# The first stage of a hybrid S5, attention and expert layer: a hand-laid order on three engines, whole fp32 operands in four projections, chunk products with swapped operands, and other pages

## The chip, the cores and the metric

The kernel runs on one core of a Trainium2 chip. The metric is the device time of one execution in microseconds (us). TensorE (PE, and PEld for its weight loads) does products and transposes, VectorE (DVE), ScalarE (ACT) and GpSimd (POOL) do elementwise work, and SyncE (SP) issues nearly all DMAs, in program order.

## The reference

One layer over 256 latent and 256 context tokens of width 1024. Cut to what matters here:

```python
# h = modulated RMSNorm; one projection, columns [S5 input 512 | K 128 | V 128 | Q 512 | gates 2048]
ug  = u.reshape(b, l, 32, 16)                       # 32 groups of 16 channels
bu  = einsum('blgp,gnp->blgn', ug, bbar)            # 64 complex states per group
h   = diag_scan(lbar, bu, h0, reverse)              # both directions, context state carried over
y  += einsum('blgn,gpn->blgp', h, cmat).real        # S5 read-out, then GLU
q, k = rms_normalised_and_rotated(q, k)             # 8 query heads, 2 key heads, 64 wide
attn = softmax(q k^T over latent and context keys) v
out  = (sigmoid gates merge both branches) @ w_out  # gated residual add
# sub-layer 2: modulated RMSNorm, top 4 of 32 experts, clamped SwiGLU, gated residual, final norm
```

Shift, scale and gate of both sub-layers come from one product of SiLU(c) with `w_mod` (1024 x 6144).

## The kernel before, in words

SBUF holds 24 pages of 1 MB (`pg0` to `pg23`). `load` (L90) issues a DMA on SP's queue and keeps program order, so the weights form one stream; a page is loaded again after `release` or `used`, when its last reader has ended. The experts at the end are 32 x 12 such pages.

The first stage, up to the expert blocks, goes like this. Two kinds of product are used. `mm` takes fp32 operands whole. `mm3` (L83) takes operands that `split` has parted into a high and a low fp32r half (ACT copies the high half at L62, DVE subtracts at L63) and makes three products. Transposes are L86.

1. The context and latent activations `hT` are modulated and split into `hH`, `hL`. U, the S5 input projection, has 32 products of 128x256 (4 column blocks, 2 sequences, 4 k-tiles) with whole operands, k < 4, and 32 split ones, k >= 4. K and V (`kv_proj`, 32 products of 128x256) and Q (`q_proj`, 16 products of 128x512) are split.
2. `v_tables`, `w_tables` and `scan_multipliers` build the S5 tables on DVE. `v_transposes` turns the tables on PE.
3. U goes through two rounds of 16 transposes (A, then U's scan layout), each with four copies on DVE. Then eight chunk steps: `chunk_in` does four products of 64x256 and a copy on ACT, and `chunk_T` turns the result with four transposes and copies it out with two half-height copies on DVE and two on ACT. `scan_up` and `scan_steps` are the scan on DVE.
4. A loop over u = 0 to 15 does one half of a gate column block each (`gate_mm`, 24 products of 128x256; `gate_split` supplies its weights), one tile of the modulation (`mod_tile`, four products of 32x512 with one page of `w_mod`, after which `mod_load` fills the page again), one `k_kernel` (24 small products of the S5 convolution kernel; a copy to `R` after each four), from u = 4 on one unit of attention (`attn`), and other pieces at set places (`P_...`). After the last `k_kernel`, at u == 7, `R` is written to DRAM (`Rd`, 8 DMAs). At u == 9 `kernel_in` reads it back as a block Toeplitz table `Kt` (16 DMAs). `readout` at u == 11 and 12 needs `Kt`.

The 16 modulation tiles use two pages in turn, 23 and 16: eight tiles stand ahead of the loop, eight in u = 0 to 7. A scheduler orders the instructions; `strict["on"]` pins PE's order to the program's from just ahead of the loop on (L1155), `strict["vec"]` that of DVE and ACT from the output projection on. The two functions that move most:

```python
    def mod_tile(reload=True):
        ...
        if reload:
            mod_load(p_)
...
    def kernel_in():
        for hf in range(2):
            for i in range(8):
                load(Kt[hf][16 * i:16 * i + 16],
                             Rd[:, 16 * hf:16 * hf + 16, 16 * (7 - i):16 * (7 - i) + 128])
```

Of the kernel before, what the change touches and what calls it, by code (L numbers as in the profile page):

```python
# [29 lines left out]
P_QT, P_K, P_M, P_A, P_S, P_RO, P_RT, P_GL, P_B, P_BS, P_BL, P_BP = 1, 0, 10, 4, 9, 11, 13, 15, 1, 3, 1, 3  # L30
# [3 lines left out]
def hybrid_block(ctx: ExitStack, tc: tile.TileContext, a: dict, out: bass.AP):  # L34
    nc = tc.nc
    V, S, G, T = nc.vector, nc.scalar, nc.gpsimd, nc.tensor
    SP = nc.sync

# [323 lines left out]
    def split_h(k, s, eng):  # L362
        split(hT[s][:, k:k + 2], hH[s][:, k:k + 2], hL[s][:, k:k + 2], eng)

    def mod0_rows(c):
        m0 = pg(9, 1024 + 256 * c, 256)
        V.tensor_copy(m0, pm0[c][:, 0:256])  # L367
# [176 lines left out]
    mod_load(23)  # L544


    Vt = [pg(p_).rearrange("p (g r m) -> p g r m", g=8, r=2) for p_ in (22, 2, 3, 14)]
    vpage = [8, 9, 8, 9]
# [42 lines left out]
    WR, WI = [], []  # L591

    def w_tables(qt):
        gs = slice(8 * qt, 8 * qt + 8)
        td = pg((19, 11, 12, 3)[qt], 0, 1024).rearrange("p (g j k) -> p g j k", g=8, j=8)
        for r, tab in ((0, WR), (1, WI)):
            tab.append(pg((18, 19, 11, 12)[qt], 1024 * r, 1024).rearrange("p (g j k) -> p g j k", g=8, j=8))
# [7 lines left out]
        V.tensor_mul(WR[qt], cc(0), lw(0))  # L605
        V.tensor_mul(td, cc(1), lw(1))
        V.tensor_add(WR[qt], WR[qt], td)
        V.tensor_mul(WI[qt], cc(1), lw(0))
        V.tensor_mul(td, cc(0), lw(1))
        V.tensor_sub(WI[qt], WI[qt], td)  # L610
# [25 lines left out]
    renew(12, "r")
    renew(11, "r")
    wuh, wul = [pg(p_).rearrange("p (k f) -> p k f", k=4) for p_ in (12, 11)]
    for k in range(4):
        split(wu[1][:, k], wuh[:, k], wul[:, k], V)  # L640
    last = mod0_rows(1)
    del held["m", 0], held["m", 1]
    with tc.issue_after(last.ins):
        v_tables(0)
        v_tables(1)
        scan_multipliers()
    u_proj(0)
    u_proj(1)
# [5 lines left out]
    u_proj(2)
    for s_ in range(2):
        for k in (0, 2):
            split_h(k, s_, V)
# [7 lines left out]
    v_tables(3)
    v_transposes(2)

    kv_ps, q_ps = [], []

    def kv_proj(i):  # L670
        b = bank(("kv", i))
        for t in range(2):
            for k in range(8):
                ts_ = slice(128 * t, 128 * t + 128)
                mm3(b[:, 256 * t:256 * t + 256], hH[i][:, k, ts_], hL[i][:, k, ts_], wkvh[:, k], wkvl[:, k],
                    k == 0, k == 7)
        kv_ps.append(b)
# [67 lines left out]
    for i in range(8):  # L745
# [4 lines left out]
        if i % 2:  # L750
            mod_tile()
# [983 lines left out]
```

## Time and profile before

| | |
|---|---|
| median of 3 runs | 1284.38 us (1282.16 to 1284.6) |
| profiled execution | 1285.06 us, its span 1283.4 us |
| mean granted TensorE clock | 0.981 |
| PE busy | 1167.6 us (91%) |
| DVE busy | 424.4 us (33%) |
| ACT busy | 197.3 us (15%) |
| DMA | 462.56 MB, mean 360 GB/s |
| chain that ended last | PE 44%, DMA 43%, DVE 9% |

The span runs from the first to the last instruction of the profiled execution; 1.66 us lie around it. Busy shares are means over stages with different limits, so a change in the first stage is read from that stage alone. In the rows, x is a count of instructions, and "idle before" is the idle time of an engine just ahead of a group with the work that ended it.

### The profile page before, as it was taken

The page shows a single profiled execution, that of the slowest core. Times are in us where ns is not written, and L with a number is a line of the kernel's source. Part 1 is how long each engine was busy: PE and PEld are TensorE (multiplying, and loading weights), DVE is VectorE, ACT ScalarE, POOL GpSimd, SP SyncE. Part 2 cuts the span into 40 slices and gives each one's busy share as a digit, 9 for nine tenths or more (in the row PEclk, how much of TensorE's full clock was granted, in tenths as well). Part 3 has the DMA queues.
Part 4 walks back from the last instruction along what each step waited for, and adds up shares of the span by engine and source line. Part 5 has one row for each costly group of instructions (what it writes and reads, how often), then busy time and mean ns, then how long its engine had stood idle before and what let it go on. Part 6 is the DMA issues. An engine that isn't in the chain of part 4 may idle for free.

```text
span 1283.4 us, 16161 instructions
## 1 busy us (share of the span) xinstructions
PE 1167.6 (91%) x6711; PEld 538.0 (42%) x6712; DVE 424.4 (33%) x923; ACT 197.3 (15%) x372; POOL 39.1 (3%) x47
## 2 busy tenths in 40 slices
PE   3889698899999999999999898989898989999986
PEld 2667477788543333333333232323232323233224
DVE  5999998474321112211121111211111111111211
ACT  3334346441110000000000000000000000000001
POOL 1130100011000000000000000000000000000000
PEclk9899899899999999999999999999999999999998
DMA  9934479679899999999999999999999999999996
GB/s 281 291 105 158 169 259 175 192 268 367 313 417 417 418 417 417 416 416 417 417 416 418 417 418 418 417 417 417 418 416 416 417 416 416 416 417 416 417 386 197
DMA packets 123104, 462.56 MB, mean 360 GB/s; under 512 B 20669, under 2 KB 46953, under 8 KB 88210
## 3 DMA queue, kind: packets, MB, share of 16 engines
q1 hardware_dynamic: 122562, 460.90, 92.3%
q8 instruction: 55, 0.90, 0.3%
q0 software_dynamic: 416, 0.56, 0.1%
q14 instruction: 23, 0.19, 0.0%
q10 hardware_dynamic: 48, 0.01, 0.0%
HBM read 459.89 MB, written 1.54 MB: 360 GB/s over the span
## 4 chain that ended last, share of the span: by engine, by line
PE 44%; DMA 43%; DVE 9%; issue 2%; SPq 1%; ACT 1%; POOL 0%; DVEq 0%; POOLq 0%; ACTq 0%
PE bk L83 41%; DMA pg<-in_w_gate_up_dram 30%; DMA pg<-in_w_down_dram 11%; PE bk L86 3%; DVE pg L63 2%; DMA pg<-Rd 2%; SPq L90 1%; DVE pg L853 0%; DVE pg L851 0%; DVE pg L854 0%; DVE pg L565 0%; DVE pg L568 0%; DVE pg L566 0%; DVE pg L564 0%; DVE pg L844 0%
## 5 line engine op out<-in xcount | busy, mean ns | idle before, releaser
L83 PE MATMUL bk<-pg,pg 128*64 128x512 f32 (+6 forms) x5344 | 996.4, 477 | 69.0 <-DMA pg<-in_w_down_dram 28.1
L83 PEld LDWEIGHTS bk<-pg,pg 128*64 128x64 f32 (+3 forms) x5344 | 447.4, 154 | 554.7 <-issue 349.9
L1472 DVE TENSOR_SCALAR pg<-bk 128x512 f32<-128x512 f32 x32 | 22.1, 692 | 291.2 <-PE bk L83 291.2
L1383 DVE TENSOR_TENSOR pg<-bk,shT 128x512 f32<-128x512 f32 x32 | 22.1, 692 | 266.4 <-PE bk L83 266.4
L86 PE MATMUL bk<-ident,pg 128*128 128x128 f32 x480 | 79.9, 292 | 18.6 <-DVE pg L367 4.2
L86 PEld LDWEIGHTS bk<-ident,pg 128*128 128x128 f32 x480 | 54.4, 145 | 85.8 <-issue 46.2
L1505 DVE TENSOR_TENSOR pg<-bk,pg 128x512 f32<-128x512 f32 x30 | 20.7, 691 | 189.2 <-PE bk L83 189.2
L1484 ACT ACTIVATE pg<-bk 128x256 f32<-128x256 f32 x32 | 12.3, 383 | 396.2 <-PE bk L86 396.2
L83 PE MATMUL bk<-pg 64*128 64x512 f32 (+1 forms) x368 | 70.4, 485 | 0.0
L1489 ACT ACTIVATE pg<-bk 128x512 f32<-128x512 f32 x32 | 19.1, 596 | 258.1 <-PE bk L86 258.1
L63 DVE TENSOR_TENSOR pg<-pg,pg 128x512 fp32r<-128x512 f32 (+3 forms) x63 | 50.6, 817 | 18.4 <-ACT pg L62 16.3
L62 ACT ACTIVATE pg<-pg 128x512 fp32r<-128x512 f32 (+3 forms) x63 | 44.0, 721 | 51.4 <-PE bk L83 40.7
L1473 ACT ACTIVATE pg<-pg 128x512 f32<-128x512 f32 x32 | 20.1, 629 | 186.1 <-DVE pg L1472 186.1
L83 PEld LDWEIGHTS bk<-pg 64*128 64x128 f32 (+1 forms) x368 | 19.9, 160 | 50.2 <-issue 50.2
L83 PE MATMUL bk<-pg,selB 128*64 128x512 bf16 (+1 forms) x196 | 33.9, 383 | 0.0
L83 PE MATMUL bk<-pg,scond 128*32 128x256 f32 (+1 forms) x256 | 28.6, 519 | 0.8 <-DMA pg<-in_w_mod_dram 0.6
L1589 POOL DMA_DIRECT2D pg<-g2d x2 | 1.3, 642 | 883.8 <-PE bk L83 883.8
L1474 DVE TENSOR_SCALAR pg<-bk 128x512 f32<-128x512 f32 x32 | 22.1, 692 | 5.3 <-PE bk L83 5.3
L1476 DVE SCALAR_TENSOR_TENSOR pg<-pg 128x512 f32<-128x512 f32 x32 | 22.1, 692 | 1.1
L1475 DVE TENSOR_TENSOR pg<-pg 128x512 f32<-128x512 f32 x32 | 21.8, 682 | 1.9 <-ACT pg L1473 1.8
L1480 DVE TENSOR_SCALAR pg<-iot,posp,gate 128x128 f32<-128x128 f32 x64 | 18.9, 339 | 0.0
L1373 DVE TENSOR_SCALAR pg<-iot,posp,rs 128x64 f32<-128x64 f32 x64 | 15.7, 306 | 0.1
(294 smaller groups left out, 422.5 us busy)
## 6 DMA issues: line engine op xcount, KB each, us to landing
pg<-in_w_gate_up_dram SPq DMA_DIRECT2D x256, 1024.0 KB, 20.0
pg<-in_w_down_dram SPq DMA_DIRECT2D x127, 1024.0 KB, 20.0
pg<-in_w_mod_dram SPq DMA_DIRECT2D x16, 1024.0 KB, 5.4
pg<-in_w_in_dram SPq DMA_DIRECT2D x13, 1024.0 KB, 7.3
pg<-in_w_mod_dram SPq DMA_DIRECT2D x16, 512.0 KB, 9.0
pg<-in_w_out_dram SPq DMA_DIRECT2D x4, 1024.0 KB, 11.9
pg<-Rd SPq DMA_DIRECT2D x16, 128.0 KB, 8.5
pg<-in_w_ssm_out_dram SPq DMA_DIRECT2D x2, 1024.0 KB
```

The lines of the kernel that those rows point to most:

```text
L62: S.activation(hi.bitcast(F32R), src, AF.Copy)
L63: eng.tensor_sub(lo.bitcast(F32R), src, hi)
L83: pinned(T.matmul(*ar, **kw))
L86: pinned(T.transpose(*ar))
L1383: pv_(V.tensor_add(xg[p % 2][:, 4 * half:4 * half + 4], pb.rearrange("p (k m) -> p k m", k=4), shk[:, 4 * half:4 * half + 4].unsqueeze(2). ...
L1472: pv_(V.tensor_scalar(gx, pgate, 7.0, None, op0=ALU.min))
L1473: pa_(S.activation(sx, gx, AF.Sigmoid, scale=1.702))
L1474: pv_(V.tensor_scalar(ux, pup, 7.0, -7.0, op0=ALU.min, op1=ALU.max))
L1475: pv_(V.tensor_mul(gx, gx, sx))
L1476: pv_(V.scalar_tensor_tensor(ux, ux, 1.0, gx, op0=ALU.add, op1=ALU.mult))
L1489: pa_(S.activation(dst, pmx, AF.Copy))
L1505: pv_(V.tensor_mul(yx, pdn, g2h))
```

## The change

PE, DVE and ACT keep the program's order from the U projection on (`Pinned`). U, K, V and Q use whole fp32 operands, so the splits of `wu[1]`, `wkv`, `wq` and of the context activations go; `hH` and `hL` remain for the latents, for the gates. A chunk is sixteen products of 64x64 whose operands are swapped, so that the scan layout comes out at once; `chunk_T` goes, and one copy each on DVE and ACT remains. The copies after the A and U transposes move from DVE to ACT. The modulation uses one page at a time (10 for the first six tiles, 15 for the last ten); six tiles stand ahead of the loop and ten in u = 0 to 9. The loop does two `k_kernel` in each of u = 0 to 3, rotates Q and K at u = 0 and 1, does `scan_up` at u == 2 and the scan's pieces in u = 3 to 8, writes `Rd` at u == 3 and reads it at u == 5 (before 7 and 9). Other pages are renamed to fit.

```diff
-P_QT, P_K, P_M, P_A, P_S, P_RO, P_RT, P_GL, P_B, P_BS, P_BL, P_BP = 1, 0, 10, 4, 9, 11, 13, 15, 1, 3, 1, 3
+P_QT, P_M, P_A, P_SU, P_S, P_RO, P_RT, P_GL, P_B, P_BS, P_BL, P_BP = 2, 10, 4, 3, 9, 11, 13, 15, 1, 3, 1, 3
...
+    V, S = Pinned(nc.vector), Pinned(nc.scalar)
...
-    hH, hL = [[pg(p_).rearrange("p (k t) -> p k t", k=8) for p_ in ps] for ps in ((13, 0), (10, 1))]
+    mod_load(10)
...
+    hH, hL = [pg(p_).rearrange("p (k t) -> p k t", k=8) for p_ in (0, 1)]
...
-    mod_load(23)
...
-            o = ub[q][:, 256 * s:256 * s + 256]
-            if k < 4:
-                mm(o, wu[0][:, k, f], hT[s][:, k], k == 0 and s == 0, False)
-            else:
-                mm3(o, wuh[:, k - 4, f], wul[:, k - 4, f], hH[s][:, k], hL[s][:, k], False, k == 7 and s == 1)
-
-    def u_proj(q):
-        for k in range(4, 8):
-            u_mm(q, k)
+            mm(ub[q][:, 256 * s:256 * s + 256], wu[k // 4][:, k % 4, f], hT[s][:, k], k == 0 and s == 0,
+               k == 7 and s == 1)
...
+    def kv_proj(i, t):
...
+        for k in range(8):
+            mm(kv_ps[i][:, 256 * t:256 * t + 256], hT[i][:, k, 128 * t:128 * t + 128], wkv[:, k], k == 0, k == 7)
...
+    def q_proj(t):
+        b = bank(("q", t))
+        for k in range(8):
+            mm(b, hT[1][:, k, 128 * t:128 * t + 128], wq[k // 4][:, k % 4], k == 0, k == 7)
...
+    def a_transposes():
...
+                S.activation(A[:, h, :, 4 * j4:4 * j4 + 4], b.rearrange("p (j g k) -> p g j k", j=4, g=8), AF.Copy)
...
+                S.activation(U[:, 4 * g4:4 * g4 + 4, :, h], b.rearrange("p (g q c) -> p g q c", g=4, q=4), AF.Copy)
...
+    def chunk(i):
...
+        for j in range(4):
+            g = 4 * i + j
+            for r in range(2):
+                for d in range(2):
+                    rhs = U[:, g % 8, g // 8]
+                    mm(b[64 * d:64 * d + 64, 128 * j + 64 * r:128 * j + 64 * r + 64],
+                       Vt[g // 8][:, g % 8, r, 64 * d:64 * d + 64], rhs[:, :, ::-1] if d else rhs, True, True)
+        bv = b.rearrange("p (g r h c) -> p h c r g", g=4, r=2, h=2)
+        V.tensor_copy(vv[0][:, :, :, 4 * i:4 * i + 4], bv[:, 0])
+        S.activation(vv[1][:, :, :, 4 * i:4 * i + 4], bv[:, 1], AF.Copy)
...
+    strict["on"] = strict["vec"] = True
+    for k in range(3):
         for q in range(4):
             u_mm(q, k)
         mod0_mm(1, k)
...
+    mod0_mm(1, 3)
+    mod0_copy(1)
...
+    v_tables(0)
+    v_tables(1)
+    for k in (4, 5):
+        for q in range(4):
+            u_mm(q, k)
...
-    split(wkv, wkvh, wkvl, V)
...
+    v_tables(2)
+    v_tables(3)
+    scan_multipliers()
+    for q in range(4):
+        u_mm(q, 6)
+        u_mm(q, 7)
+        u_out(q)
+    kv_proj(0, 0)
+    a_transposes()
     v_transposes(0)
-    v_tables(2)
-    u_proj(3)
...
-    split(wq[0], wqh[0], wql[0], V)
...
+    for i in range(8):
+        if i in (4, 6):
+            v_transposes(i // 2)
+        chunk(i)
+        if i == 1:
+            release(22)
+        if i == 2:
+            S.activation(hH.bitcast(F32R), hT[1], AF.Copy)
+        if i < 3:
+            w_tables(1)
+        elif i == 3:
+            V.tensor_sub(hL.bitcast(F32R), hT[1], hH)
+        else:
+            w_tables(2)
+        if i in (3, 5):
+            mod_tile()
     mod_tile()
...
-    split(wq[1], wqh[1], wql[1], V)
-    mod_load(16)
...
-    def chunk_in(i):
-        b = bank()
-        for j in range(2):
-            for e in range(2):
-                g = 4 * i + 2 * j + e
-                mm(b[64 * e:64 * e + 64, 256 * j:256 * j + 256],
-                   U[:, g % 8, g // 8].rearrange("p h c -> p (h c)"),
-                   Vt[g // 8][:, g % 8].rearrange("p r m -> p (r m)"), True, True)
-        vo = pg(7, 512 * (i % 2), 512)
-        S.activation(vo, b, AF.Copy)
...
-    def chunk_T(i, vo):
-        b = bank()
-        for j in range(2):
-            for r in range(2):
-                ttrans(b[:, 128 * (2 * r + j):128 * (2 * r + j) + 128],
-                            vo[:, 256 * j + 128 * r:256 * j + 128 * r + 128], ident)
-        for h in range(2):
-            bv = b.rearrange("p (r g h c) -> p h c r g", r=2, g=4, h=2)[:, h]
-            V.tensor_copy(vv[h][0:64, :, :, 4 * i:4 * i + 4], bv[0:64])
-            S.activation(vv[h][64:128, :, :, 4 * i:4 * i + 4], bv[64:128, ::-1], AF.Copy)
...
-    for qt in range(4):
-        w_tables(qt)
...
+    kv_proj(0, 1)
+    mod_tile(False)
+    kv_proj(1, 0)
+    kv_proj(1, 1)
+    w_tables(4)
...
+    gate_split(0, 0)
+    gate_split(0, 1)
+    used("gate", 0)
+    q_proj(0)
+    q_proj(1)
+    mod_load(15)
+    w_tables(24)
...
     renew(14, "r")
+    renew(21, "r")
...
-            mm3(gbk[0][:, 256 * j:256 * j + 256], wgh[:, j, k], wgl_[:, j, k], hH[1][:, k], hL[1][:, k], k == 0, k == 7)
-        if i < 7:
-            gate_split(i + 1, j)
+            mm3(gbk[0][:, 256 * j:256 * j + 256], wgh[:, j, k], wgl_[:, j, k], hH[:, k], hL[:, k], k == 0, k == 7)
...
-    R = pg(22, 0, 1920).rearrange("p (g m) -> p g m", g=8)
+    R = pg(19, 0, 1920).rearrange("p (g m) -> p g m", g=8)
...
-    Kt = [pg(p_).rearrange("p (g m) -> p g m", g=16) for p_ in (6, 9)]
...
+    Kt = [pg(p_).rearrange("p (g m) -> p g m", g=16) for p_ in (6, 19)]
...
-    strict["on"] = True
-    gate_split(0, 0)
-    gate_split(0, 1)
-    used("gate", 0)
-    scan_up()
+    def next_split(u):
+        if u < 16:
+            gate_split(u // 2, u % 2)
+            if u % 2:
...
     n_attn, n_scan = 0, 0
     for u in range(16):
+        if u > 1:
+            next_split(u + 1)
+        if u == 2:
+            scan_up()
+        if P_SU <= u < P_S:
+            s1 = len(pieces) * (u + 1 - P_SU) // (P_S - P_SU)
+            scan_steps(n_scan, s1)
+            n_scan = s1
         gate_mm(u // 2, u % 2)
         if mods["done"] < 16:
-            p_ = mod_tile()
+            mod_tile()
             if mods["done"] == 16:
-                release(23)
-        i = u // 2 + 1
-        if u % 2 and i < 8 and not (where["gate", i] == 20 and state["next"] >= 8):
-            used("gate", i)
+                release(15)
+        if u < 4:
+            k_kernel(2 * u)
+            k_kernel(2 * u + 1)
+        if u == 0:
+            rope_q()
+            next_split(2)
+        if u == 1:
+            rope_k()
+            q_split()
         if u == P_QT:
             for i in range(2):
                 q_T(i)
                 k_T(i)
-        if P_K <= u < 8 + P_K:
-            k_kernel(u - P_K)
-        if u == 7 + P_K:
+        if u == 3:
             Rd = dpool.tile([16, 32, 240], F32, name="Rd")
             for q in range(4):
                 for e in range(2):
                     load(Rd[:, 8 * q:8 * q + 8].rearrange("p (g e) m -> p e g m", e=2)[:, e],
                                 R[32 * q + 16 * e:32 * q + 16 * e + 16].rearrange("p (g e) m -> p e g m", e=2)[:, e])
+        if u == 5:
+            kernel_in()
...
         if u == P_S:
             scan_out()
-            kernel_in()
-        if u < P_S:
-            s1 = len(pieces) * (u + 1) // P_S
-            scan_steps(n_scan, s1)
-            n_scan = s1
```

On SP's queue, at the end of the modulation's loads (`w_mod`), the program before reads like this (`in_w_in` is a page of gate weights, `Rd` the S5 kernel's way through DRAM):

```order
47 L90 DMA pg23_83<-in_w_mod_dram 128x2048
48 L90 DMA pg3_63<-in_b_gate_up_dram 32x1024 x3
49 L90 DMA pg16_76<-in_w_mod_dram 128x2048
50 L90 DMA pg20_80<-in_w_in_dram 128x8x256
51 L90 DMA pg23_83<-in_w_in_dram 128x8x256
52 L90 DMA pg15_75<-in_w_in_dram 128x8x256
53 L90 DMA Rd_1909<-pg22_82 16x4x240 x8
54 L90 DMA pg3_63<-in_b_down_dram 32x1024 x3
55 L90 DMA pg6_66<-Rd_1909 16x16x128 x8
56 L90 DMA pg9_69<-Rd_1909 16x16x128 x8
57 L90 DMA pg23_83<-in_w_glu_dram 128x4x512
```

and the changed program, at the same place of SP's queue:

```order
38 L104 DMA pg15_75<-in_w_mod_dram 128x2048 x2
39 L104 DMA Rd_1515<-pg19_79 16x4x240 x8
40 L104 DMA pg23_83<-in_w_in_dram 128x8x256
41 L104 DMA pg15_75<-in_w_mod_dram 128x2048
42 L104 DMA pg3_63<-in_b_gate_up_dram 32x1024 x3
43 L104 DMA pg15_75<-in_w_mod_dram 128x2048
44 L104 DMA pg6_66<-Rd_1515 16x16x128 x8
45 L104 DMA pg19_79<-Rd_1515 16x16x128 x8
46 L104 DMA pg22_82<-in_w_in_dram 128x8x256
47 L104 DMA pg15_75<-in_w_mod_dram 128x2048 x2
```

Before, all modulation loads stand ahead of the write and the 16 reads of `Rd`; now five loads of the loop stand behind the write, three of them behind the reads too (row 47, and one more further on), and all go to one page.

On PE, in the last chunks and the projections, the program before reads (`pg17` holds U, `pg7` a chunk's first result, `bk` is a PSUM bank):

```order
300 L83 MATMUL bk2_979<-pg22_82,pg17_77 64x256 x4
301 L86 MATMUL bk3_985<-ident_126,pg7_67 128x128 x4
302 L83 MATMUL bk5_999<-pg2_62,pg17_77 64x256 x4
303 L86 MATMUL bk7_1005<-ident_126,pg7_67 128x128 x4
304 L83 MATMUL bk0_1014<-pg13_309,pg0_306 128x512
305 L83 MATMUL bk0_1014<-pg10_308,pg0_306 128x512
306 L83 MATMUL bk0_1014<-pg13_309,pg1_307 128x512
```

and the changed program, from the last two chunks to the first half of Q:

```order
128 L97 MATMUL bk4_905<-pg17_77,pg21_81 64x64 x16
129 L97 MATMUL bk6_926<-pg17_77,pg21_81 64x64 x16
130 L97 MATMUL bk7_664<-pg10_70,scond_161 32x512 x4
131 L97 MATMUL bk5_607<-pg14_74,pg2_62 128x256 x8
132 L97 MATMUL bk7_664<-pg10_70,scond_161 32x512 x4
133 L97 MATMUL bk0_964<-pg14_74,pg3_63 128x256 x16
134 L97 MATMUL bk1_996<-pg15_75,pg3_63 128x512 x4
135 L97 MATMUL bk1_996<-pg16_76,pg3_63 128x512 x4
```

The three products of split halves became one whole product per k-tile, the transposes between the chunks went, and the modulation tiles (`scond`) all read page 10 here, the last two of the six with eight products of 128x256 between.

## Rows read from the trace of the kernel before

**Rows 1.** Page, section 2: 40 slices of 32.1 us, tenths busy and GB/s.

```profile
DVE  5999998474321112211121111211111111111211
...
GB/s 281 291 105 158 169 259 175 192 268 367 313 417 417 418 417 417 416 416 417 417 416 418 417 418 418 417 417 417 418 416 416 417 416 416 416 417 416 417 386 197
```

**Rows 2.** Windows: window, length, busy PE, PEld, DVE, ACT, POOL; clock, DMA share, GB/s.

```profile
160.00:200.00 40.00, 35.73 (x554) 27.13 (x552) 38.50 (x97) 21.01 (x39) 1.89 (x2) 0.96 0.78 258
240.00:280.00 40.00, 39.98 (x364) 35.37 (x354) 30.45 (x58) 22.56 (x47) 1.60 (x2) 1.00 0.85 304
```

**Rows 3.** Chain that ended last: start, length, what.

```profile
51.25 2.50 DVE pg L63 x4
...
210.65 10.48 DMA pg<-Rd 
221.14 9.14 DMA pg<-Rd 
...
597.72 20.75 DMA pg<-in_w_down_dram 
```

**Rows 4.** Timeline of PE: start, length, line, out<-in, shape, count, idle before.

```profile
31.81 3.69 PE L83 MATMUL bk<-pg,pg 128*128 128x256 f32 x16 [1.36 <-issue]
...
98.72 6.21 PE L83 MATMUL bk<-pg,pg 128*128 128x256 f32 x48
...
107.60 1.95 PE L83 MATMUL bk<-pg,pg 128*64 128x256 f32 x16
...
122.43 6.74 PE L83 MATMUL bk<-pg,pg 128*128 128x512 f32 x32
...
147.11 2.93 PE L83 MATMUL bk<-pg,pg 128*128 128x256 f32 x12 [10.21 <-DVE pg L63]
...
158.68 2.40 PE L86 MATMUL bk<-ident,pg 128*128 128x128 f32 x20
...
169.44 1.06 PE L83 MATMUL bk<-pg,scond 128*32 128x512 f32 x8
170.44 0.64 PE L83 MATMUL bk<-pg,pg 64*32 64x112 f32 x32
...
192.63 3.12 PE L83 MATMUL bk<-pg,pg 128*128 128x256 f32 x24
...
206.00 3.57 PE L83 MATMUL bk<-pg,pg 128*128 128x256 f32 x26
...
230.32 8.93 PE L83 MATMUL bk<-pg,pg 128*32 128x128 f32 x118 [7.65 <-DMA pg<-Rd]
...
239.62 6.35 PE L83 MATMUL bk<-pg,pg 128*32 128x128 f32 x122
```

**Rows 5.** Lines by form, 0 to 330 us: busy, mean ns, idle before.

```profile
L63 DVE TENSOR_TENSOR pg<-pg,pg 128x512 fp32r<-128x512 f32 x46 | 30.6, 684 | 16.2 <-ACT pg L62 14.2 <-PE bk L83 1.9
...
L63 DVE TENSOR_TENSOR pg<-pg,pg 128x2048 fp32r<-128x2048 f32 x3 | 6.8, 2279 | 0.0
...
L564 DVE TENSOR_TENSOR pg<-pg,pg 128x1024 f32<-128x1024 f32 x4 | 4.9, 1214 | 0.0
```

**Rows 6.** SP's queue: its timeline, DMA issues (count, KB, us to landing), PE's waits.

```profile
201.67 4.11 SPq L90 DMA_DIRECT2D Rd<-pg  x8
...
207.29 14.15 SPq L90 DMA_DIRECT2D pg<-Rd  x16
222.55 0.39 SPq L90 DMA_DIRECT2D pg<-in_w_glu_dram  x1
...
pg<-in_w_mod_dram SPq DMA_DIRECT2D x16, 1024.0 KB, 5.4
...
pg<-in_w_glu_dram SPq DMA_DIRECT2D x1, 1024.0 KB, 10.2
...
PE bk L83 <- DMA pg<-in_w_mod_dram: 0.6, 1, 0.6
```

**Rows 7.** Window of 5 us just behind that wait, columns as in rows 2.

```profile
230.00:235.00 5.00, 4.68 (x88) 4.32 (x90) 0.00 (x0) 0.00 (x0) 0.00 (x0) 0.50 0.36 131
```

More of the change, by code (lines that the diff above doesn't have):

```diff
@@ L543, in hybrid_block @@
     order.close()
[L544 to L548 removed]
+    Vt = [pg(p_).rearrange("p (g r m) -> p g r m", g=8, r=2) for p_ in (22, 18, 19, 21)]
+    vpage = [20, 11, 4, 13]
     def v_part(qt, r):
@@ L603, in lw, with all_w, w_tables @@
             return LW[:, r, :, gs].rearrange("p t g -> p g t").unsqueeze(3).to_broadcast([128, 8, 8, 16])
[L605 to L610, printed above, removed]
+        yield V.tensor_mul(WR[qt], cc(0), lw(0))
+        yield V.tensor_mul(td, cc(1), lw(1))
+        yield V.tensor_add(WR[qt], WR[qt], td)
+        yield V.tensor_mul(WI[qt], cc(1), lw(0))
+        yield V.tensor_mul(td, cc(0), lw(1))
+        yield V.tensor_sub(WI[qt], WI[qt], td)
+    def all_w():
+        for qt in range(4):
+            yield from w_steps(qt)
+    w_left = all_w()
+    def w_tables(n):
+        for _ in range(n):
+            next(w_left, None)
     uT = pg(17).rearrange("p (h j q c) -> p h j q c", h=2, j=8, q=4)
@@ L629, in u_proj, with u_out @@
+    def u_out(q):
         S.activation(uT[:, :, :, q], ub[q].rearrange("p (h c j) -> p h j c", h=2, j=8), AF.Copy)
         del held["u", q]
-    for k in range(4):
+    kv_ps, q_ps = [], []
+    def kv_proj(i, t):
+        if t == 0:
+            kv_ps.append(bank(("kv", i)))
+        for k in range(8):
[4 more added lines that the diff above has]
+            mm(b, hT[1][:, k, 128 * t:128 * t + 128], wq[k // 4][:, k % 4], k == 0, k == 7)
+        q_ps.append(b)
@@ new lines, in hybrid_block @@
+    A = pg(12).rearrange("p (h g j k) -> p h g j k", h=2, g=8, j=8)
+    def a_transposes():
+        for h in range(2):
+            for j4 in range(2):
+                b = bank()
+                for j in range(4):
+                    ttrans(b[:, 128 * j:128 * j + 128],
+                           uT[:, h, 4 * j4 + j].rearrange("p q c -> p (q c)"), ident)
+                S.activation(A[:, h, :, 4 * j4:4 * j4 + 4], b.rearrange("p (j g k) -> p g j k", j=4, g=8), AF.Copy)
+    U = pg(17).rearrange("p (g q h c) -> p g q h c", g=8, q=4, h=2)
@@ new lines, in u_transposes @@
+    def u_transposes():
+        for h in range(2):
+            for g4 in range(2):
+                b = bank()
+                for g in range(4):
+                    ttrans(b[:, 128 * g:128 * g + 128], A[:, h, 4 * g4 + g].rearrange("p j k -> p (j k)"), ident)
+                S.activation(U[:, 4 * g4:4 * g4 + 4, :, h], b.rearrange("p (g q c) -> p g q c", g=4, q=4), AF.Copy)
+    vv = [pg(p_).rearrange("p (s r g) -> p s r g", s=32, r=2) for p_ in (8, 9)]
+    def chunk(i):
+        b = bank()
+        for j in range(4):
+            g = 4 * i + j
[7 more added lines that the diff above has]
+        S.activation(vv[1][:, :, :, 4 * i:4 * i + 4], bv[:, 1], AF.Copy)
@@ L635, in hybrid_block @@
         mod0_mm(1, k)
[L636 to L648, printed above, removed]
-    c_transposes()
-    renew(4, "r")
-    renew(21, "r")
-    wkvh, wkvl = [pg(p_).rearrange("p (k f) -> p k f", k=8) for p_ in (4, 21)]
@@ L653, in hybrid_block @@
-    split(wkv, wkvh, wkvl, V)
[L654 to L657, printed above, removed]
+    mod0_mm(1, 3)
+    mod0_copy(1)
+    u_mm(0, 3)
+    u_mm(1, 3)
+    mod0_T(1)
+    mod0_rows(1)
+    u_mm(2, 3)
+    u_mm(3, 3)
+    v_tables(0)
[3 more added lines that the diff above has]
+            u_mm(q, k)
+    c_transposes()
+    v_tables(2)
[5 more added lines that the diff above has]
+        u_out(q)
@@ L658, in hybrid_block @@
+    kv_proj(0, 0)
+    a_transposes()
     v_transposes(0)
-    v_tables(2)
-    u_proj(3)
     mod_tile()
-    renew(11)
-    renew(12)
+    u_transposes()
     v_transposes(1)
[L665 to L677, printed above, removed]
@@ L744, in hybrid_block @@
-    prev = None
-    for i in range(8):
-        vo = chunk_in(i)
-        if prev is not None:
-            chunk_T(i - 1, prev)
-        prev = vo
-        if i % 2:
-            mod_tile()
-        if i in (2, 4):
-            q_proj(i // 2 - 1)
-    chunk_T(7, prev)
-    for qt in range(4):
-        w_tables(qt)
-    release(20)
-    renew(4)
+    mod_tile()
+    for i in range(8):
[14 more added lines that the diff above has]
+            mod_tile()
```

140 lines of the change are left out of this document (62 added, 78 removed).

## The prediction

> **What bounds the kernel now.** Look first at the page's slices [rows 1]: from the twelfth (353 us) almost to the end the GB/s line stands at 416 to 418 GB/s, so the expert blocks are paced by their weights. In the chain of waits this is told again: from 597.7 us on its long pieces are weight loads [rows 3]. That stream can fill only pages which the first stage has freed, and in 240 to 280 us PE is busy 39.98 of 40 us [rows 2]. So there is no slack behind the first stage: I take a shift of its last part as a shift of the end, one for one.
>
> What bounds the first stage changes on the way. PE works to 51.25 us, where the chain passes to DVE's splits [rows 3]. Later PE waits 10.21 us for DVE to split the first gate weights, and starts the loop at 147.11 [rows 4]. In 160 to 200 us DVE is busy 38.5 of 40 [rows 2]. Last comes the S5 kernel's way through DRAM: SP issues the 16 reads of `Rd` from 207.29 [rows 6], they land in 210.65 to 230.28 by the chain [rows 3], and PE, idle 7.65 us, starts the read-out at 230.32 [rows 4]. That read-out is my mark: what it shifts by, the end shifts by.
>
> **PE's work ahead of the loop.** A whole product of 256 columns is two instructions in the trace, 2 x 3.69 / 16 = 0.46 us; in three parts it is 3 x 6.21 / 48 = 0.39 [rows 4]. U's second half and K and V have 32 products each: 32 x 0.07 = 2.3 us more, twice. A split product of 512 columns is 3 x 6.74 / 32 = 0.63 [rows 4]; a whole one isn't in the trace. Below it is bounded by 0.63 (no dearer than split), above by twice the narrow one, 0.92. I take 0.92, since it is the same kind of instruction with twice the columns: Q 16 x 0.29 = 4.6 more. Together 9.2 us more on PE.
>
> A chunk was four products, 1.95 / 2, and four transposes of 2.40 / 20 = 0.12: 1.46 us [rows 4]. Now it is 32 instructions of 64 columns. The small products of the S5 kernel bound them below, 0.64 / 32 = 0.02 each or 0.64; a transpose's 0.12 each, 3.9, above. By columns (half of those of a 128-column transpose, or a quarter of a 256-column product at 0.23) they come to 1.0 to 2; I take 1.3, so eight chunks cost 10.4. The ends are 5.3 us less and 20 more.
>
> Count PE from 51.5 us in the new order, where U's first half is done as before: U's rest 32 x 0.46 = 14.7, 104 transposes x 0.12 = 12.5, K and V 14.7, chunks 10.4, six modulation tiles of 1.0 (four products, 1.06 [rows 4]) = 6.0, Q 14.7. That is 73.0, or 124.5 us.
>
> DVE no longer stands before PE there. It loses 12 subtractions of 0.68 and 3 of 2.28, gains one of 2.28 [rows 5], and gives eight copies to ACT, each at a 512-wide operation's 0.68: 8.2 + 6.8 - 2.3 + 5.4 = 18 us less. Its four `v_tables`, 24 operations of 1.21 [rows 5] = 29 us, stand ahead of most else and are done at about 85; PE asks for the last at about 104. The whole operands thus buy DVE's time with PE's.
>
> **One modulation page.** With two pages in turn PE waited 0.6 us in all for `w_mod` [rows 6]. A load takes 5.4 us from issue to landing [rows 6], and with one page it can be issued only when the tile before has been read. Ahead of the loop five reloads have 22.5 us of PE work between them, in unequal pieces: 5 x 5.7 (with 0.3 for the hand-over) - 22.5 = 6 us of waiting. The loop so begins at 130.5, 16.6 earlier than 147.11. The Trainium skill (Trainium Kernel Development and Optimization, Best Practices) asks for double buffers, so that a load lies beside the work on the buffer before. The 0.6 us with two pages agree; by that rule this part is a loss, and by the rows it is 6 us.
>
> **The loop to u = 4.** A step of PE is 3.12 for the gate, 1.06 for the tile, and now two `k_kernel` of about 0.9 (0.64 and a third of that again for the narrow products) [rows 4]: 6.0. But DVE has a fixed order: Q's rotation (8 operations of 0.68 = 5.4), six gate and Q splits (4.1), `scan_up` (four operations of 1.21, four of 0.68 and shorter ones, 9.2 [rows 5]), and some 40 narrow ones between, about 8. That is 26.7, to 157; only then come the copies of the Q and K transposes, behind which PE's gate for u = 3 stands. So u = 3 begins at 159 and ends at 165, u = 4 at 170. The last copy to `R` is done at about 167.4. `Rd` is written in 4.1 us of issuing [rows 6]; behind it stand a gate page and the load for u = 5's tile. At 417 GB/s a page is 2.6 us on the queue, so tile 5 lands about 180 and ends at **181.5**.
>
> **The reads of `Rd`.** Now comes the term that decides. `kernel_in` is issued at u = 5, behind the load for tile 6 (issued at 181.5, landing at 187). The reads take 19.6 us in the chain [rows 3], some 2 MB at 105 GB/s: to **207**. The load for tile 7 can be issued only after tile 6, so it stands in the queue behind all 16 reads, and a gate page too: 207 + 2 x 2.6 = **212.3**. PE has u = 6 and u = 7's gate to do meanwhile, two short pieces, and then sits idle for about 20 us; before, all tiles were loaded ahead of the reads. What queues behind them is late, as the row for `w_glu` shows: issued at 222.55, landed 10.2 us later, not 5.4 [rows 6].
>
> Then tile 7, after idleness at the low clock (two of the 1.06: it ends at 214.3), and four steps to u = 11's read-out. The profile's steps from 192.63 to 206.00 are 13.4 for two [rows 4], or 6.7 each: 214.3 + 4 x 6.65 = **240.9**, which is 10.6 later than 230.32. One thing comes back. Before, PE came to the read-out from idleness: granted clock 0.50, the lower of its two levels, in 230 to 235 [rows 7], and its first 118 instructions took 8.93 us where the next 122 took 6.35 [rows 4], 2.6 us. That goes, as `Kt` is there long before. Sum: +10.6 - 2.6 = **+8.0**, 1285.06 + 8.0 = 1293.1. The median of the runs lies 0.7 below the profiled execution, so I say **1292**. The unknown of Q (4.6 lower at best) and the cheap end of the chunks (5.3) would begin the loop earlier, but DVE's order to 157 takes most of that up; the likeliest case's own range is 1286 to 1298.
>
> **Rivals.** *The reads don't hold the queue* (faster). SP's queue feeds many engines; if the load for tile 7 passes beside the reads, PE goes on from u = 5 at 6.6 us a step: 181.5 + 6 x 6.9 = 223, minus 2.6 for the clock and 7.3 for the read-out: 9.9 less, **1275**. It decides if a load issued behind the reads lands before they end. Against it is the `w_glu` row, which shows half of such a delay; for it, that the load landed in 10.2, not in 20. The Trainium skill (DMA: Bandwidth & Descriptors, Queues, rings and completion order) says that each DMA engine takes descriptors in its ring's order, but that completions come in no order over engines; the first half speaks for the stall, the second for this rival. Chance 0.2.
>
> *DVE is quicker to 157.* If the 40 narrow operations and the waits between cost little, u = 3 to 5 go at PE's pace, tile 5 ends 8 us earlier, and with the same stall the sum is +0: 1282 to 1286, **1284**. It speaks for it that I guessed the narrow ones; against it that DVE was the full engine there [rows 2]. Chance 0.2.
>
> *The hand order is worse than the scheduler's.* If the chunks lie halfway to their dear end (+5), or a later piece of the scan stands before what PE wants, 5 to 10 us are added: **1299**. For it: three engines wait for one another in a fixed order with no leeway. Chance 0.1.
>
> *The stream hides the slip.* That the expert blocks absorb it would give 1284 again; 39.98 of 40 us on PE and 417 GB/s behind it [rows 1, 2] leave nothing to absorb, and I fold its few hundredths into the second rival.
>
> **How the numbers follow.** My forecast has 0.5, the rivals 0.2, 0.2 and 0.1. About 0.2%, 2.6 us, is what a measurement of this kernel can tell from no change. Slower by more: 0.5, the last rival's 0.1 and a little of the second: 0.62. Faster: 0.2 and the second rival's lower end: 0.28. Same: 0.10. The predicted time is that of the likeliest, 1292; the range goes from 1272, the fast rival with half of the chunks' cheap end, to 1300.
>
> **What would show it.** Right: the loop begins near 131, a whole 512-column product takes 0.9 us, tile 5 ends near 181, PE shows one wait for `w_mod` of some 20 us beside the reads of `Rd`, and the read-out begins near 241 at full clock; behind it the blocks keep their times. Wrong: the longest wait for `w_mod` is under 8 us, or the read-out begins before 228; then the queue does not hold what I say, or DVE's order lets PE through.

## The result and the profile after

The changed kernel takes 1322.91 us (median of 4 runs, 1318.05 to 1323.7) against 1284.1 for the one before: 1.0297 times as long, 95% interval 1.027 to 1.0324. The forecast was 1292, range 1272 to 1300. The direction was right, the size was not. The profiled execution took 1322.63 us with a span of 1321.0, 37.6 more than before.

Slices of the page (40 of 33.0 us), which answer to [rows 1]:

```profile
GB/s 277 309 161 96 141 182 207 98 267 195 318 349 397 416 416 417 417 417 418 417 418 417 417 418 416 417 416 417 418 417 418 417 418 418 416 417 416 416 387 197
```

The weight stream reaches 416 in the fourteenth slice (429 us) instead of the twelfth (353), and runs at the same rate behind. So the loss lies in the first stage, as forecast. Two windows, which answer to [rows 2], show in what state that stage is:

```profile
160.00:200.00 40.00, 28.76 (x264) 22.11 (x262) 26.45 (x64) 15.68 (x30) 0.95 (x1) 0.84 0.68 156
240.00:280.00 40.00, 31.12 (x376) 27.52 (x376) 22.59 (x41) 18.38 (x38) 1.32 (x3) 0.90 0.52 180
```

Before, DVE was busy 38.5 us in the first window and PE 39.98 in the second. Now no engine is full in either window, and over the whole of each the DMA engines aren't either (0.68 and 0.52). What the engines wait for is told below. PE's timeline, which answers to [rows 4]:

```profile
79.12 3.95 PE L97 MATMUL bk<-pg,pg 128*64 128x64 f32 x128
...
106.67 23.78 PE L97 MATMUL bk<-pg,pg 128*128 128x256 f32 x88
130.38 1.06 PE L97 MATMUL bk<-pg,scond 128*32 128x512 f32 x8
...
143.81 5.37 PE L97 MATMUL bk<-pg,pg 128*128 128x256 f32 x24 [3.58 <-ACT pg L49]
...
160.81 3.91 PE L97 MATMUL bk<-pg,pg 128*128 128x256 f32 x24
...
185.19 1.94 PE L97 MATMUL bk<-pg,scond 128*32 128x512 f32 x8 [4.26 <-DMA pg<-in_w_mod_dram]
...
215.25 1.94 PE L97 MATMUL bk<-pg,scond 128*32 128x512 f32 x8 [17.34 <-DMA pg<-in_w_mod_dram]
...
244.70 4.71 PE L97 MATMUL bk<-pg,pg 128*128 128x256 f32 x24 [4.10 <-ACT pg L49]
...
252.97 6.35 PE L97 MATMUL bk<-pg,pg 128*32 128x128 f32 x122
...
298.86 3.65 PE L97 MATMUL bk<-pg,pg 128*64 128x256 f32 x14 [5.91 <-DVE pg L49]
...
310.40 29.85 PE L97 MATMUL bk<-pg,pg 128*128 128x256 f32 x206
```

The loop's first modulation tile is at 130.38, behind a gate of 3.1, so the loop begins at 127.3, 19.8 earlier than before. The wait at u = 7, 17.34 us for `w_mod`, is the forecast one. But the read-out (its first half, at u = 11) begins at 252.97, 22.65 later than the 230.32 of [rows 4], and PE still waits for ACT and DVE behind it. At 310.40 the products of the branches begin. The chain of waits shows how far that goes:

```profile
253.04 6.28 PE bk L97 x122
...
310.64 33.49 PE bk L97 x224
...
390.41 1.11 PE bk L100 x4
```

In the chain before, the piece behind the last attention step begins at 276.65, and the first expert block's transposes behind DVE's work at 353.84:

```profile
276.65 13.59 PE bk L83 x112
...
353.84 0.66 PE bk L86 x4
```

From the two traces: read-out +22.65, less 2.6 for its clock; to 310.64, +34.0; to 390.41, +36.6; the end +37.6. So about 14 us are lost between read-out and branches, and 2.6 in the first expert block, where I had assumed a plain shift.

Who waits there is told by the waits of DVE and ACT in 160 to 312 us (engine and line, waited for; us, times, longest):

```profile
DVE pg L49 <- ACT pg L49: 28.4, 30, 2.1
DVE smx L49 <- PE bk L97: 18.9, 7, 10.4
DVE ssum L49 <- ACT pg L49: 13.5, 16, 0.8
...
ACT pg L49 <- DVE smx L49: 52.7, 16, 14.8
ACT pg L49 <- DVE pg L49: 22.2, 19, 4.4
```

DVE waits 41.9 us for ACT, and ACT 74.9 for DVE. The kernel before, in the same piece of work (160 to 278 us), has these:

```profile
DVE pg L63 <- ACT pg L62: 16.0, 7, 11.1
DVE ssum L1006 <- ACT pg L1005: 3.1, 6, 1.4
...
ACT pg L62 <- PE bk L83: 15.6, 11, 3.0
ACT pg L1005 <- DVE smx L1003: 9.6, 9, 2.8
...
ACT pg L845 <- DVE pg L844: 4.4, 5, 1.4
```

With the smaller rows that aren't shown, DVE waited 20.7 us for ACT there and ACT 20.9 for DVE. In 10 of the 16 softmaxes (`ssum`: DVE waits for ACT's exponentials) DVE had no such wait; now it has one in all 16, 0.84 us each. Part of the 52.7 us is the stall at tile 7 itself (14.8, the longest); where that stall is gone (the run **Both** below) they are still 39.7. A piece of the timelines of ACT and DVE in the change, at u = 9, shows the same in the small:

```profile
240.61 0.63 ACT L49 ACTIVATE pg<-pg 128x512 bf16<-128x512 f32 x1
242.00 0.63 ACT L49 ACTIVATE pg<-pg 64x512 bf16<-64x512 f32 x1 [0.76 <-DVE pg L49]
243.38 1.79 ACT L49 ACTIVATE pg<-pg 32x512 bf16<-32x512 f32 x3 [0.76 <-DVE pg L49]
...
241.28 0.69 DVE L49 TENSOR_TENSOR pg<-pg,pg 64x512 f32<-64x512 f32 x1 [1.30 <-ACT pg L49]
242.66 0.69 DVE L49 TENSOR_TENSOR pg<-pg,pg 32x512 f32<-32x512 f32 x1 [0.69 <-ACT pg L49]
244.68 1.29 DVE L49 TENSOR_TENSOR pg<-pg,pg 128x512 fp32r<-128x512 f32 x2 [1.33 <-ACT pg L49]
```

These are the bias parts, a chain that goes to and fro between the two. They are needed only by the experts, but the split of the next gate weights stands behind them (the last two of the three ACT operations and the last DVE row), and PE waits 4.10 us for it at 244.70.

### The profile page after: what moved, and what is told of

Read it like the earlier page. It is cut to its first block, busy times and chain, and to the rows that moved or that the text cites. A ratio compares the mean times of both kernels' runs of the same rounds, so it can differ in the third digit from the quotient of the medians.

```text
span 1321.0 us, 16216 instructions
## 1 busy us (share of the span) xinstructions
PE 1175.6 (89%) x6791; PEld 542.7 (41%) x6792; DVE 414.2 (31%) x893; ACT 182.2 (14%) x350; POOL 31.5 (2%) x47
## 4 chain that ended last, share of the span: by engine, by line
PE 47%; DMA 38%; DVE 8%; ACT 2%; SPq 2%; issue 1%; ACTq 0%; DVEq 0%
PE bk L97 45%; DMA pg<-in_w_gate_up_dram 27%; DVE pg L49 7%; DMA pg<-in_w_down_dram 6%; DMA pg<-in_w_mod_dram 4%; ACT pg L49 2%; SPq L104 2%; PE bk L100 2%; DMA pg<-Rd 1%; DMA rows<-in_norm_g_dram 0%; DVE smx L49 0%; DVE LS L49 0%; ACT L49 0%; ACTq L49 0%; DVE gate L49 0%
## 5 line engine op out<-in xcount | busy, mean ns | idle before, releaser
L97 PE MATMUL bk<-pg,pg 128*64 128x512 f32 (+6 forms) x5456 | 1005.4, 471 | 70.9 <-DMA pg<-in_w_down_dram 29.6
L49 ACT ACTIVATE pg<-bk 128x512 f32<-128x512 f32 (+4 forms) x154 | 76.4, 521 | 763.3 <-PE bk L100 685.6
L49 DVE TENSOR_TENSOR pg<-pg,pg 128x1024 f32<-128x1024 f32 (+9 forms) x144 | 123.2, 884 | 31.8 <-ACT pg L49 30.5
L49 ACT ACTIVATE pg<-pg 128x512 f32<-128x512 f32 (+9 forms) x118 | 76.8, 671 | 255.2 <-DVE pg L49 237.9
L49 DVE TENSOR_TENSOR pg<-bk,pg 128x512 f32<-128x512 f32 (+4 forms) x52 | 32.1, 619 | 227.8 <-PE bk L97 223.9
L100 PE MATMUL bk<-ident,pg 128*128 128x128 f32 x448 | 72.9, 292 | 14.1 <-DVE pg L49 6.7
L97 PE MATMUL bk<-pg,scond 128*32 128x256 f32 (+1 forms) x256 | 30.0, 564 | 32.7 <-DMA pg<-in_w_mod_dram 32.7
L97 PEld LDWEIGHTS bk<-pg 64*128 64x128 f32 (+1 forms) x368 | 19.8, 159 | 50.0 <-issue 50.0
L49 DVE TENSOR_TENSOR pg<-pg 128x512 f32<-128x512 f32 (+3 forms) x89 | 37.4, 435 | 3.9 <-ACT pg L49 3.1
L49 DVE SCALAR_TENSOR_TENSOR pg<-pg 128x512 f32<-128x512 f32 (+3 forms) x67 | 30.3, 459 | 6.4 <-DMA pg<-in_x_dram 4.7
L49 ACT ACTIVATE pg<-bk,smx 128x512 f32<-128x512 f32 x16 | 11.0, 687 | 52.7 <-DVE smx L49 52.7
L49 DVE TENSOR_REDUCE smx<-bk 128x1 f32<-128x512 f32 x16 | 11.0, 686 | 18.9 <-PE bk L97 18.9
```

The source lines that it names most:

```text
L49: i = f(*ar, **kw)
L97: pinned(T.matmul(*ar, **kw))
L100: pinned(T.transpose(*ar))
```

## The experiments

The theories: **queue**, the single modulation page and the reads of `Rd` in SP's queue cost some 20 us; **order**, the fixed order on DVE and ACT costs some 26 (9 ahead of the read-out, 14 behind it, 3 in the first expert block). Against the first: these waits only cover what DVE and ACT would take anyway. Against the second: one badly placed item, or the shorter lead of the gate split. "Ratio" is to the kernel before, with its 95% interval.

**The reads of `Rd` later** (from the change):

```diff
-        if u == 5:
+        if u == 8:
             kernel_in()
```

> kernel_in (the 16 reads of Rd) is issued at u = 8 instead of u = 5, all else as in the change. Theory of the queue: the load for tile 7 no longer stands behind the reads, so PE's wait of 17.3 us for w_mod goes, with some 2 us of low clock; the read-out, 2 steps later, still finds Kt there or waits under 5 us for it; read-out at 231 to 236 instead of 253, time 1303 to 1307. Rival (the fixed order on VectorE and ScalarE paces these steps, so the wait only hides theirs): the read-out comes under 8 us earlier, time above 1313.

Measured 1310.44 us, ratio 1.0219 (1.0186 to 1.0252). The read-out begins at 241.96, 11.0 earlier. The 17 us wait is gone, but waits of 4.5, 5.4 and 5.0 us for `w_mod` stay in every second step, where a gate page stands ahead of the load. Between the two theories' numbers: the queue is a cause, and one page by itself another.

**The reads on another queue** (from the change):

```diff
-                load(Kt[hf][16 * i:16 * i + 16],
+                G.dma_start(Kt[hf][16 * i:16 * i + 16],
```

> kernel_in stays at u = 5, but its 16 reads are issued on GpSimd's DMA queue. Theory of the queue's order: the w_mod load for tile 7 lands in 5 to 8 us, the wait falls from 17.3 to under 5, time 1303 to 1309. Rival (the DMA engines are full of the small pieces of Rd, whoever issues them): the load still takes over 12 us beside the reads, wait over 8 us, time above 1313.

Measured 1326.15 us, ratio 1.0332 (1.0304 to 1.036): the rival. Two loads of `w_mod` in the chain of waits (start, length):

```profile
178.42 14.47 DMA pg<-in_w_mod_dram
...
194.93 13.52 DMA pg<-in_w_mod_dram
```

They are the loads for tiles 5 and 6, and PE waits for both, while tile 7 now waits only 0.17:

```profile
192.94 1.93 PE L97 MATMUL bk<-pg,scond 128*32 128x512 f32 x8 [11.21 <-DMA pg<-in_w_mod_dram]
...
208.50 1.94 PE L97 MATMUL bk<-pg,scond 128*32 128x512 f32 x8 [8.45 <-DMA pg<-in_w_mod_dram]
...
215.42 1.07 PE L97 MATMUL bk<-pg,scond 128*32 128x512 f32 x8 [0.17 <-DMA pg<-in_w_mod_dram]
```

Issued from GpSimd, the reads begin 10 us sooner, at 177.2, as soon as `R` is written, and run beside both loads, each of which takes some 14 us instead of 5.3. The load for tile 7 no longer stands behind them, but the stall has only moved: the waits for `w_mod` from 120 us on are 27.3 us, 27.6 in the change. In 177 to 208 us the share of the DMA engines is 1.01, so they are full at 193 GB/s. SP's order decides which tile waits; that one waits comes from the engines' time that the reads take, whoever issues them. The Trainium skill (DMA: Bandwidth & Descriptors, Rules for kernel authors) says that spreading DMAs over issuing engines gives no bandwidth, since all run on the same 16 DMA engines; the two rows of the chain agree.

**A second modulation page**, from u = 2 on (from the change):

```diff
         if u == P_QT:
             for i in range(2):
                 q_T(i)
                 k_T(i)
+            mod_load(16)
```

> The modulation gets a second page from u = 2 on (16, which is empty between the Q transposes and the gates' second half), pages 15 and 16 in turn; kernel_in stays at u = 5. Theory of the queue: the loads for tiles 5 to 7 stand ahead of the reads, the one for tile 8 still stands behind them; the waits for w_mod fall from 32.7 to 10 to 16 us, the read-out comes 10 to 15 us earlier, time 1306 to 1313. Rival (one page is no loss, the reads alone are): the waits stay above 25 us, time above 1317.

Measured 1310.23 us, ratio 1.0207 (1.019 to 1.0225). The waits for `w_mod` fall from 32.7 to 15.5 us with those ahead of the loop (in the loop from 27.6 to 8.5), one of them 7.7 at tile 8, as expected, and the read-out comes at 240.46.

**Both** (the second page, and `kernel_in` at u = 7):

> Second page as in the run before, and kernel_in at u = 7, behind the last load of the modulation. Theory of the queue and the page: no wait for w_mod above 2 us in the loop, read-out at 228 to 236 instead of 253, time 1297 to 1306, under the 1310 of kernel_in at u = 8 with one page by 5 to 13. Rival (the order on VectorE and ScalarE paces these steps by itself): waits for the gate's split take their place, time above 1307.

Measured 1314.18 us, ratio 1.025 (1.0234 to 1.0267): no better than either alone, and the rival's number. The wait for `w_mod` is down to 1.1 us, but PE now waits 11.5 us for a gate split ahead of 223.74. The chain of waits ahead of that:

```profile
204.97 8.58 DMA pg<-Rd
...
213.61 5.93 DMA pg<-in_b_down_dram
...
219.64 0.64 ACT pg L49
...
220.31 0.70 DVE pg L49
...
221.03 0.64 ACT pg L49
```

The load that now stands behind the reads is that of a bias. Nobody needs it soon, but in the fixed order its parts on ACT and DVE stand ahead of the gate split. With the queue mended for `w_mod`, the order handed the delay of another load on to PE. What the fixed order would cost with this load ahead of the reads too was not run.

**DVE and ACT not pinned** ahead of the output projection, and behind it as before (from the change):

```diff
-    V, S = Pinned(nc.vector), Pinned(nc.scalar)
+    V, S = nc.vector, nc.scalar
...
-        return i
+        return tc.keep_in_program_order(i) if strict["vec"] else i
...
-    strict["on"] = strict["vec"] = True
+    strict["on"] = True
...
+    strict["vec"] = True
     warm(AF.Sqrt, ssum[:, 15:16])
```

> VectorE and ScalarE are not pinned ahead of the output projection, and from there on only where the kernel before pins them; PE's order and all else as in the change. Theory of the order: the wait at tile 7 stays (15 to 20 us), but from the read-out to the output projection it takes about 30 us as before instead of 44, the first expert block loses 3 us less, and 5 to 9 us come back ahead of the read-out; time 1294 to 1303. Rival (the gate weights are now split one step ahead instead of two, which no order mends): waits for the split stay, time above 1313.

Measured 1296.47 us, ratio 1.0119 (1.0083 to 1.0155): 26 us less than the change, the theory's number. The wait at tile 7 stays, 14.7 us. The 26 us are a balance: without the fixed order the loop begins at 139.2 instead of 127.3, so ahead of the loop that order gains 11.9 us. At tile 7 nothing of this is left (it begins at 214.16, in the change at 215.25).

**Unpinned from u = 6 to the output projection only**, all pinned again behind it:

> As the change up to u = 5; VectorE and ScalarE are unpinned from u = 6 to the output projection, and all pinned again behind it. Theory of the order: 14 us behind the read-out and part of the 9 us ahead of it come back, the 3 us in the first expert block don't; time 1300 to 1308. Rival (the order ahead of u = 6 is what costs): under 5 us come back, time above 1317.

Measured 1299.06 us in 2 runs, ratio 1.0121 (1.0087 to 1.0154), 1 us under the theory's range. Three rows of PE, tile 7, the read-out and the branches:

```profile
213.88 1.94 PE L97 MATMUL bk<-pg,scond 128*32 128x512 f32 x8 [13.61 <-DMA pg<-in_w_mod_dram]
...
242.90 6.36 PE L97 MATMUL bk<-pg,pg 128*32 128x128 f32 x122
...
286.42 16.94 PE L97 MATMUL bk<-pg,pg 128*128 128x256 f32 x138
```

From tile 7 to the read-out it takes 29.0 us, in the change 37.7, and from there to the branches 43.5, in the change 57.4. So, with the stall at tile 7 in place, almost all of the 26 us lie between u = 6 and the output projection; the 6.1 us wait in the first expert block stays here and is 3.3 where that block is pinned as before.

**Both causes taken away**: the second page, `kernel_in` at u = 7, and the fixed order on DVE and ACT ending at u = 2, with the earlier pins from the output projection on:

```diff
     for u in range(16):
+        if u == 2:
+            strict["hand"] = False
```

> Second page and kernel_in at u = 7, and the fixed order on VectorE and ScalarE ends at u = 2; free up to the output projection, from there on pinned where the kernel before pins. Both causes taken away: loop begins at 127 as in the change, 24 to 28 us for the order and 17 to 25 for page and reads come back of 39: time 1268 to 1280, faster than the kernel before. Rival (the two overlap, what one gives the other has already given): 1284 to 1296.

Measured 1267.76 us, ratio 0.9887 (0.9866 to 0.9908): 16 us faster than the kernel before, 55 faster than the change. Two windows as above, the two halves of the read-out on PE's timeline, and the waits of DVE and ACT in 160 to 261 us:

```profile
160.00:200.00 40.00, 36.95 (x356) 28.82 (x356) 34.60 (x82) 23.79 (x44) 1.96 (x3) 0.96 0.95 264
240.00:280.00 40.00, 39.98 (x293) 36.06 (x292) 29.14 (x48) 17.22 (x31) 7.45 (x6) 1.00 0.73 269
```

```profile
209.06 2.83 PE L97 MATMUL bk<-pg,pg 128*32 128x128 f32 x96
...
222.10 6.36 PE L97 MATMUL bk<-pg,pg 128*32 128x128 f32 x122
```

```profile
DVE ssum L49 <- ACT pg L49: 4.0, 8, 0.8
...
ACT pg L49 <- DVE smx L49: 14.8, 10, 3.1
```

PE is full again in the second window (39.98 of 40). The read-out's first half begins at 209.06 and its second at 222.10, 21.3 and 17.5 earlier than before (230.32 and 239.62 [rows 4]), and the span ends 17.4 earlier. ACT's wait for the softmax maxima has fallen from 52.7 to 14.8 us.

**The fourth corner**, order ended at u = 2, page and reads as in the change:

> The fixed order on VectorE and ScalarE ends at u = 2 as in the 1268 us version, but with the change's one modulation page in the loop and kernel_in at u = 5. It fills the fourth corner: change 1323, page and reads mended 1314, both mended 1268. If the two costs add up, this is 1268 + 9 = 1277. If each hides behind the other while both are there, it is 1289 to 1299, beside the 1296 and 1299 of the two unpinned runs.

Measured 1289.67 us, ratio 1.0055 (1.0037 to 1.0073). Page and reads are worth 9 us under the full fixed order (1323 to 1314) and 22 without it (1290 to 1268); the order is worth 33 with them and 46 once they are mended. Each cause stood in front of a part of the other, the second of the two cases that were expected.

**The order ended at u = 6 instead of 2, and at the loop's start**, both with page and reads mended:

> Second page and kernel_in at u = 7, fixed order on VectorE and ScalarE up to u = 6 instead of 2, then free. If the order costs only where attention, biases and the later pieces meet (u = 6 on): 1268 to 1273. Rival (it costs in u = 2 to 5 too, where TensorE waited 3.6, 5.4 and 2.7 us): 1275 to 1285.

> As the 1268 us version, but the fixed order on VectorE and ScalarE ends at the loop's start. The scheduler may move the gates' split and the scan ahead of Q's rotation: TensorE's wait of 6.4 us at u = 2 goes, 1262 to 1267. Rival (it spreads work that is urgent there): 1268 to 1275.

The first: 1285.68 us, ratio 1.0011 (0.9996 to 1.0025), the rival's side, 0.7 above its range: with the queue mended, u = 2 to 5 under the fixed order cost 18 us. The second: 1270.17, ratio 0.9889 (0.9868 to 0.9911): no different from ending it at u = 2, and so the rival's range. The wait of 6.4 us at u = 2 is gone, but in 110 to 420 us PE's waits for ACT rise from 3.4 to 8.0 and those for `w_mod` from 3.7 to 6.0. So the fixed order costs nothing in u = 0 and 1.

**The gate split placed sooner in the fixed order**, with page and reads mended, and alone:

```diff
-        if u > 1:
-            next_split(u + 1)
...
+        if u:
+            next_split(u + 2)
         if u < 4:
             k_kernel(2 * u)
```

> VectorE and ScalarE pinned all the way as in the change, second page and kernel_in at u = 7 (1314 so far), and one thing moved in the fixed order: the split of the next gate weights stands right behind step u's gate products instead of behind that step's attention and biases. If the place of the splits is what the order costs: the waits of TensorE for the split (28.6 us for ScalarE's copies) fall under 12, time 1285 to 1298. Rival (two engines that take turns in a fixed order cost it, whatever is moved): waits turn up elsewhere, time above 1306.

> The change with that one move alone. The wait for tile 7 (17 us) stays and covers part of it: time 1305 to 1316 if the place of the splits matters; rival: within 4 us of 1323.

Measured 1315.33 us (ratio 1.025, 1.0233 to 1.0267) and 1320.71 (1.0289, 1.0272 to 1.0307): the rival in both. The waits turn up elsewhere: in the first PE's waits for ACT fall from 28.6 to 18.1 us, but those for DVE rise from 7.2 to 16.9, and PE waits 13.2 us once, for an ACT that waits 11.0 for the same late bias. So it isn't this one place that costs it. Whether another fixed order could do as well as the free one wasn't tried.

**Parts of the change alone, in the kernel before.** First the chunk: `chunk_in` and `chunk_T` replaced by the change's `chunk`.

> The kernel before with one part of the change alone: chunks of sixteen 64x64 products with swapped operands, no transposes, one copy each on VectorE and ScalarE. From the rows a chunk falls from 1.46 us to 3.95 / 4 = 0.99 on TensorE, and VectorE loses eight copies; VectorE is the full engine there. If that stretch sets the end: 2 to 4 us less, 1280 to 1282. Rival (the wait for Rd behind it, or a split, takes it up): within 1 us of before.

Measured 1277.45 us, ratio 0.996 (0.9944 to 0.9976): 6 us faster, more than expected. Then Q with whole operands as well (its splits dropped, `release(15)` and `mod_load(16)` moved behind `q_proj`). In this run the page of `hT[1]` has been written with an S5 table when Q reads it, so Q is another product of the same shape:

> The kernel before with swapped chunk operands (1277.5) and Q with whole operands: eight splits of 512 columns go (5.4 us of VectorE, 5 of ScalarE), TensorE pays 16 x 0.21 = 3.4 us more (0.84 a product in the change's trace, 0.63 before). VectorE paces the stretch: 1272 to 1276. Rival (TensorE paces it): 1279 to 1282.

Measured 1270.54 us, ratio 0.9891 (0.9868 to 0.9914): 7 us faster again, more than the 2 to 5 expected. These parts of the change are gains where DVE paces the stretch: in 150 to 200 us it is busy 48.5 of 50 before, and 49.4 in both runs.

## Why the prediction was wrong

**What held.** A chunk took 3.95 / 4 = 0.99 us (forecast 1.3), a whole product of Q 0.87 (0.92: 13.9 us of busy time for 16), the waits for one page ahead of the loop 1.33 + 1.19 + 1.08 + 1.28 = 4.9 (6). The loop began at 127.3 (130.5), u = 3 at 160.8 (159), tile 5 ended at 187.1 (181.5), tile 7 began at 215.25 (212.3), its wait was 17.3 (20). Up to u = 7 the sum was within 6 us everywhere. And "the whole operands thus buy DVE's time with PE's" was borne out by the parts run alone.

That the sum stayed so near at tile 7 is in part luck. These are the reads on SP's queue and the load for tile 7 in the chain:

```profile
187.58 14.28 SPq L104 DMA_DIRECT2D pg<-Rd  x16
```

```profile
203.75 11.46 DMA pg<-in_w_mod_dram
```

The sum lets the reads begin when tile 6's load has landed, 5.5 us behind tile 5's end. They were issued right behind that load instead, which made up for the 5.6 us by which tile 5 was late. It then gives them 19.6 us, the two pieces of the chain in [rows 3]. From the first issue to the last landing they took 22.5 us (the last was issued at 201.55 and landed 8.5 later, at 210.1), and 23.0 in the kernel before too (207.29 [rows 6] to 230.28). That term was 3 us short, and tile 7 was 3 us late. Smaller slips change little: two steps of 13.37 us are 6.69 each, a 1 MB page at 417 GB/s is 2.5 us, and the first rival's step is 6.6 in one place and 6.9 in the other, 2 us of its 1275.

**What failed, first: the steps behind tile 7.** The sum took "four steps" of 6.65 us, a price read from 192.63 to 206.00 of the kernel before [rows 4]. There DVE and ACT ran in an order of the scheduler's. Under the fixed order the same work took from 215.25 to 252.97, 37.7 instead of 28.6; with DVE and ACT freed from u = 6 on it took 29.0.

**What failed, second: "what it shifts by, the end shifts by".** I made the read-out the mark and took the rest as a shift. But the pins reach on through the gates, GELU, GLU and branches to the output projection and past it, and 14 + 3 us were lost there (from the read-out to the branches 57.4, freed 43.5). I had costed the edit that pins DVE and ACT up to u = 4 only, and put it at nothing behind. Of the 29.6 us between the +8.0 of the sum and the measured +37.6, 3 are the reads', 9 the steps', 14 lie between read-out and branches, 3 in the first expert block and 1 behind it. The third rival named the cost of the fixed order, at 5 to 10 us and a chance of 0.1; the runs show 26 to 33 alone and 46 with the queue mended. The sign to look for stood in the profile: in 240 to 280 us PE was busy 39.98, DVE 30.45 and ACT 22.56 of 40 [rows 2], with softmax, bias parts, splits and scan all between the two. My reading, which the runs show for this one order only: work that fills two engines to two thirds, in chains that cross between them, fits only if other work may step in while a chain crosses.

**The queue.** The place and the size of the stall were right, but not its worth. Taking it away gave 9 to 13 us under the fixed order, since the order's waits moved into its room. The step "the load for tile 7 can be issued only after tile 6, so it stands in the queue behind all 16 reads" was right as to when the load was issued, at 203.75. It then took 11.5 us, not 5.3, and landed at 215.2, behind the last read. Yet the reads on another queue were no better: the engines' time, not the queue alone, was what the load lacked. My first rival would have needed that free.

## What to carry to other kernels

When a change pins an engine's program order, cost it over everything that the pin reaches: list the chains that cross between pinned engines there, and count each crossing as idle time unless the program places other work between. Price steps from a trace only where the order that made it still holds. And where two causes stall the same stretch, mend both before judging either: here 9 and 33 us apart were 55 together.

## What the runs showed of the hardware

Here short waits cost TensorE twice. Behind a wait of 3.58 us the 24 gate products at 143.81 took 5.37 us instead of 3.13; the window of that stretch shows the granted clock at 0.50, the lower of its two levels:

```profile
143.80:149.00 5.20, 5.19 (x24) 5.18 (x24) 4.21 (x8) 2.39 (x5) 0.00 (x0) 0.50 0.11 24
```

The 24 products of two other gate steps took 4.90 us behind a wait of 2.67 (at 176.03) and 4.71 behind one of 4.10 (at 244.70), at granted clocks of 0.66 in 176 to 181 us and 0.64 in 244.7 to 249.2. So waits of 3 to 4 us, not only the long one, brought some 2 us each on top, and the mean clock fell from 0.981 to 0.969. And the small-piece reads of `Rd`, 2 MB, slow a 1 MB load beside them: from 5.3 us, the median, to 14.5 and 13.5 where GpSimd issues the reads, and to 11.5 beside the end of the reads on SP's own queue.
